# A choice of experts by sixteen compare-and-multiply instructions, with pinned transposes and three pairs of GpSimd work

## The chip, the cores and the metric

One core of one Trainium2 chip runs the whole program once. The metric is the device time of an execution in microseconds (us); lower is better. The kernel before took 1800.45 us, the median of three runs (1798.29 to 1802.6). Engines: TensorE (PE in the rows, PEld its weight loads), VectorE (DVE), ScalarE (ACT), GpSimd (POOL) and SyncE (SP), which issues the loads.

## What is computed

Two transformer blocks in a row over 256 tokens of width 1024. The change touches only the last part, the layer with 16384 small experts (PEER):

```python
def peer_ffn(u, w_q, sub_keys, u_tab, v_tab):      # T=256, K=16, H=8
    q = (xt @ w_q).reshape(T, H, 2, 128)
    s = jnp.einsum('thcd,hcnd->thcn', q, sub_keys)
    top_s, top_i = lax.top_k(s, K)                  # of 128 keys, per head and half c
    cand = (top_s[:, :, 0, :, None] + top_s[:, :, 1, None, :]).reshape(T, H, K * K)
    cand_i = (top_i[:, :, 0, :, None] * 128 + top_i[:, :, 1, None, :]).reshape(T, H, K * K)
    best_s, best_j = lax.top_k(cand, K)
    expert = jnp.take_along_axis(cand_i, best_j, axis=-1)
    g = jax.nn.softmax(best_s, axis=-1)
    ...
    act = gelu(einsum(xc, u_tab[ec]));  out = einsum(gc * act, v_tab[ec])
```

## The kernel before

The kernel never gathers experts. It computes the activations of all 16384 experts for all tokens, as 64 **pairs** of 256 experts (the u-loop in `peer`, lines 1534 to 1563), multiplies them by a dense weight `H` that is zero for all experts not chosen, and then runs the v-loop over 128 blocks.

**A pair** is one 1 MB load `w` (tile of `peer_u_2`), cut in two halves of 1024 columns. Each half goes through `split` (line 135): ScalarE copies it to `hi` (float32r, L145), and `lo = w - hi` (L146) is a subtraction on VectorE, or on GpSimd when `gp` is true, which in the u-loop is `i < N_POOL` (line 1539, `N_POOL = 7` at line 40). Then eight calls of `mm3` (lines 153 to 155) make three matmuls each, so a pair has 48. `hi` and `lo` have three buffers each (line 1629). The sums go to PSUM tiles `acc` for even pairs and `oa` for odd ones, two of each, so pair i+4 reuses the tile of pair i.

**The choice** (`choice`, line 1414) is a generator of 24 steps, spread over pairs 0 to 8 (lines 1532 and 1551): after pair i, steps are taken until 24(i+1)/9 are done. Steps 0 and 1 form candidates (L1422 to L1426). Steps 2 to 9 find the best 16 of 80 for 8 heads and both token halves (`topk`, L1402 to L1406). Step 10 turns places into a row place `rf` and a column place `cf` (L1437 to L1448), and casts the indices to `xb` in bf16. Step 11 makes the gate weights: L1453 subtracts, ScalarE takes the exponential (L1456), L1458 to L1460 normalise, two TensorE transposes (L1464) turn them, and L1465 to L1469 split them in three bf16 parts `g3`. It is issued after pair 4. Steps 12 to 23 look up the index at each place: for each half j of the tokens and each c of the two keys, VectorE compares 128 places with 16 numbers (L1478, 2048 columns), multiplies by the indices (L1481) and sums over 16 (L1484); TensorE transposes (L1486) and ScalarE writes a half of `iT` or `jT` (L1487).

**The weights** (`weights`, line 1490) come in 64 groups of four tokens, from pair 9 on, each with a compare `ohb` (L1495, from `jT`), four `oha` (L1498, from `iT` and `g3`), 12 small matmuls (L1505) and copies to `H` (L1512, L1514). A pair that finds n tokens of weights done multiplies these by its activations (L1547) and writes the others plainly (L1549). Pair 10 is the first for which n is not zero: it uses the first group.

The order of the instructions on each engine is not that of the program text: the tile framework lays it out beforehand by a simulated timeline (line 1749), and each engine then runs its list in order. `after(a, b)` (line 281) tells it that `a` must not stand before `b` on the same engine; nothing waits at run time for that. `peer_subkeys_2` is held in `sk`, which is last read by the last head's scores (L1526), ahead of pair 1.

Of the kernel before, what the change touches and what calls it, by code (L numbers as in the profile page):

```python
# [13 lines left out]
BF16 = mybir.dt.bfloat16  # L14
I32 = mybir.dt.int32
U32 = mybir.dt.uint32
AF = mybir.ActivationFunctionType
ALU = mybir.AluOpType
AX = mybir.AxisListType
# [17 lines left out]

N_END = 3

N_POOL = 7  # L40


class _Kernel:
# [1296 lines left out]
    def peer(self):  # L1340
        nc, I, X, V = self.nc, self.I, self.X, self.nc.vector
# [7 lines left out]
        def part(n, dt=F32):  # L1349
            o = at[0]  # L1350
            at[0] += n
            return ce[:, o:o + n].bitcast(dt) if dt is not F32 else ce[:, o:o + n]

        sk = part(2048).rearrange("p (n c) -> p n c", n=16)
        nc.sync.dma_start(sk, I["peer_subkeys_2"])
        xe = part(2048)
# [24 lines left out]
        def h_tile(first):  # L1381
            H.append((first, 32, big("H").rearrange("p (i t) -> p i t", i=32)))

        def rows_h(i, n):
            base, _, h = [z for z in H if z[0] <= i][-1]
            return h[:, i - base:i - base + n, :]
# [8 lines left out]
        xb = part(256, BF16).rearrange("p (j n a) -> p j n a", j=2, n=16)  # L1395
# [3 lines left out]
        def topk(v, ix, src):  # L1399

            scr = self.tmp([128, 128], "tk", bufs=2)[:, :src.shape[-1]]
            V.max(v[:, :8], src)  # L1402
            V.max_index(ix[:, :8], v[:, :8], src)
            V.match_replace(scr, v[:, :8], src, -3e38)
            V.max(v[:, 8:], scr)
            V.max_index(ix[:, 8:], v[:, 8:], scr)  # L1406
# [7 lines left out]
        def choice():  # L1414

            cand = xe[:, :1280].rearrange("p (j h n) -> p j h n", j=2, h=8)
            for j in range(2):
                va = v[j].rearrange("p (h c) a -> p h c a", c=2)  # L1420
                C = cand[:, j]
                V.tensor_tensor(C[:, :, :16], va[:, :, 0, 0:1].to_broadcast([128, 8, 16]), va[:, :, 1, :], op=ALU.add)  # L1422
                V.tensor_tensor(C[:, :, 16:72].rearrange("p h (a b) -> p h a b", a=7),
                                va[:, :, 0, 1:8, None].to_broadcast([128, 8, 7, 8]),
                                va[:, :, 1, None, :8].to_broadcast([128, 8, 7, 8]), op=ALU.add)
                V.tensor_tensor(C[:, :, 72:], va[:, :, 0, 8:], va[:, :, 1, 0:1].to_broadcast([128, 8, 8]), op=ALU.add)  # L1426
                yield
            bv4 = bv.rearrange("p (j h k) -> p j h k", j=2, h=8)
            bp4 = bp.rearrange("p (j h k) -> p j h k", j=2, h=8)
            for h in range(8):  # L1430
                for j in range(2):
                    topk(bv4[:, j, h], bp4[:, j, h], cand[:, j, h])
                yield

            u, rf, cf, m = [work[:, o:o + 256] for o in (0, 256, 512, 768)]
            ui = u.bitcast(U32)
            V.tensor_scalar(ui, bp, 3, None, op0=ALU.logical_shift_right)  # L1437
            V.tensor_copy(rf, ui)
            V.tensor_scalar(ui, bp, 7, None, op0=ALU.bitwise_and)
            V.tensor_copy(cf, ui)  # L1440
            V.scalar_tensor_tensor(m, rf, 9.0, cf, op0=ALU.is_equal, op1=ALU.mult)
            V.tensor_scalar(u, rf, 1.0, 8.0, op0=ALU.is_equal, op1=ALU.mult)
            V.tensor_tensor(cf, cf, u, op=ALU.add)
            V.tensor_tensor(cf, cf, m, op=ALU.subtract)
            V.tensor_scalar(rf, rf, -1.0, 0.0, op0=ALU.add, op1=ALU.max)
            V.tensor_tensor(rf, rf, m, op=ALU.add)
            for j in range(2):
                V.tensor_copy(xb[:, j], ix[j])  # L1448
            yield

            best, wt = bv.rearrange("p (n k) -> p n k", k=16), xe[:, :256]
            bw = wt.rearrange("p (n k) -> p n k", k=16)
            V.tensor_tensor(bw, best, best[:, :, 0:1].to_broadcast([128, 16, 16]), op=ALU.subtract)  # L1453
            for j in range(2):
                js = slice(j * 128, (j + 1) * 128)
                nc.scalar.activation(wt[:, js], wt[:, js], AF.Exp, scale=rs[:, j:j + 1])  # L1456
            z = self.small(16, "tk_z", bufs=1)
            V.tensor_reduce(z, bw, axis=AX.X, op=ALU.add)  # L1458
            V.reciprocal(z, z)
            V.tensor_tensor(bw, bw, z[:, :, None].to_broadcast([128, 16, 16]), op=ALU.mult)  # L1460
            pt = self.wk()[:, :256]
            for j in range(2):
                js = slice(j * 128, (j + 1) * 128)
                nc.tensor.transpose(pt[:, js], wt[:, js], self.ident)  # L1464
            nc.scalar.activation(g3[:, 0], pt, AF.Copy)  # L1465
            V.tensor_tensor(u, pt, g3[:, 0], op=ALU.subtract)
            nc.scalar.activation(g3[:, 1], u, AF.Copy)
            V.tensor_tensor(m, u, g3[:, 1], op=ALU.subtract)
            nc.scalar.activation(g3[:, 2], m, AF.Copy)  # L1469
            yield  # L1470
            eq = xe[:, 1024:].bitcast(BF16)
            eq3 = eq.rearrange("p (n s) -> p n s", s=16)
            eq4 = eq.rearrange("p (h k s) -> p h k s", h=8, k=16)
            for j in range(2):
                js = slice(j * 128, (j + 1) * 128)
                xj = xb[:, j].rearrange("p (h c) a -> p h c a", c=2)
                for c, pos in enumerate((rf, cf)):
                    V.tensor_tensor(eq3, pos[:, js, None].to_broadcast([128, 128, 16]),  # L1478
                                    self.iota[:, None, :16].to_broadcast([128, 128, 16]), op=ALU.is_equal)
                    yield  # L1480
                    V.tensor_tensor(eq4, eq4, xj[:, :, c, None, :].to_broadcast([128, 8, 16, 16]), op=ALU.mult)  # L1481
                    yield
                    hf = u[:, c * 128:(c + 1) * 128]
                    V.tensor_reduce(hf, eq3, axis=AX.X, op=ALU.add)  # L1484
                    pt = self.wk()
                    nc.tensor.transpose(pt[:, :128], hf, self.ident)  # L1486
                    nc.scalar.activation(tabs[c][:, js], pt[:, :128], AF.Copy)  # L1487
                    yield

        def weights():  # L1490

# [26 lines left out]
        for h in range(8):  # L1518
# [4 lines left out]
            s = self.wk().rearrange("p (n c) -> p n c", n=4)  # L1523
# [5 lines left out]
            if h == 1:  # L1529
                xT = self.xpair(xs, g_ffn)  # L1530
        self.e_done = self.t_done = 0
        work_, n_top, i_top, i_end, n_g = choice(), 24, 9, 62, T // 4
        done = 0
        for i in range(64):
            ut = self.next_w()
            ps = (self.acc, self.oacc)[i % 2]().rearrange("p (e t) -> p e t", e=2)
            for e in range(2):
                hi, lo = [z.rearrange("p (k e) -> p k e", k=8) for z in
                          self.split(ut[:, e * 1024:(e + 1) * 1024], gp=i < N_POOL)]
                for k in range(8):  # L1540
                    self.mm3(ps[:, e, :], (hi[:, k, :], lo[:, k, :]), (xT[0][:, k, :], xT[1][:, k, :]),
                             k == 0, k == 7)
            n = self.t_done
            h2 = rows_h(2 * i, 2)
            if n:
                nc.scalar.activation(ps[:, :, :n], ps[:, :, :n], AF.Gelu)
                V.tensor_tensor(h2[:, :, :n], h2[:, :, :n], ps[:, :, :n], op=ALU.mult)  # L1547
            if n < T:
                nc.scalar.activation(h2[:, :, n:], ps[:, :, n:], AF.Gelu)  # L1549
            self.e_done = 2 * i + 2  # L1550
            if i < i_top:
                want = n_top * (i + 1) // i_top
            else:
                want = n_top + n_g * (i + 1 - i_top) // (i_end - i_top)
            while done < min(want, n_top + n_g):
                if done == n_top:
                    for _ in work_:
                        raise AssertionError
                    h_tile(64)
                    h_tile(96)  # L1560
                    work_ = weights()
                next(work_)
                done += 1

        ps = [[self.acc() for _ in range(2)], [self.oacc() for _ in range(2)]]
# [29 lines left out]
        for i in range(128):  # L1595
# [8 lines left out]
            if i % 4 == 0:  # L1604
                ahl = self.act(F32R)
                ah, al = ahl[:, :1024], ahl[:, 1024:]
                a = rows_h(i, 4).rearrange("p i t -> p (i t)")
# [145 lines left out]
```

## Time and profile before

| | us |
|---|---|
| median of three runs | 1800.45 |
| lowest and highest | 1798.29 and 1802.6 |
| the profiled execution | 1797.24 |
| its span, first to last instruction | 1795.5 |
| TensorE busy | 1718.2 (96%) |
| VectorE busy | 982.3 (55%) |
| ScalarE busy | 683.0 (38%) |
| GpSimd busy | 309.9 (17%) |

The times in the rows are us from the start of the span. The u-loop runs from about 993 to 1430 us, the v-loop after it. In a timeline row, the first number is the start and the second the duration; successive instructions of one engine overlap a little, so the distance of two starts is what one costs its engine. Lines such as L146 or L153 are those of helpers and stand for every caller.

### The profile page before, as it was taken

To read this page: it belongs to the slowest core of one execution; us is meant where nothing else is said; L and a number is where in the kernel's file an instruction comes from. 1 tells how busy PE (TensorE), PEld (TensorE's weight loads), DVE (VectorE), ACT (ScalarE), POOL (GpSimd) and SP (SyncE) were. 2 spreads that over 40 slices of the span, in tenths; PEclk is the share of its full clock that TensorE was granted. 3 is DMA by queue.
4 is the path that set the end of the run, shared out by engine and by line. 5 is a ranking of instruction groups with operands and counts; after the bars stand their busy time and mean duration, and the time that the engine had idled before them with its cause. 6 is when DMAs were issued, how large, how long until landed. Compare 5 with 4: busy or idle time off the path is not lost. (4 is left out here: it accounts for less than half of the span.)

```text
span 1795.5 us, 27447 instructions
## 1 busy us (share of the span) xinstructions
PE 1718.2 (96%) x11096; PEld 1354.5 (75%) x11096; DVE 982.3 (55%) x2008; ACT 683.0 (38%) x1150; POOL 309.9 (17%) x178
## 2 busy tenths in 40 slices
PE   8999999999999998999999889999999999999998
PEld 7984445544434438888989889999999978888886
DVE  5462232212212116667566999999999944444444
ACT  6551121111101115546455444544444444444443
POOL 4321000000000005321537620000000022222221
PEclk9998999999999999999999989999999999999999
DMA  9527898898999978352215444444444455565553
GB/s 371 216 110 287 322 415 338 351 382 359 381 416 382 388 325 328 127 212 91 99 38 176 141 144 156 150 157 147 160 165 146 165 175 200 190 232 200 188 188 117
DMA packets 69250, 410.02 MB, mean 228 GB/s; under 512 B 9216, under 2 KB 9856, under 8 KB 28544
## 3 DMA queue, kind: packets, MB, share of 16 engines
q1 hardware_dynamic: 67840, 406.64, 60.4%
q8 instruction: 88, 1.44, 0.3%
q10 hardware_dynamic: 1280, 1.59, 0.2%
q14 instruction: 42, 0.34, 0.1%
HBM read 406.11 MB, written 2.10 MB: 227 GB/s over the span
## 5 line engine op out<-in xcount | busy, mean ns | idle before, releaser
L145 ACT ACTIVATE hi<-w 128x1024 fp32r<-128x1024 f32 x368 | 388.9, 1060 | 504.5 <-PE oa L155 176.9
L146 DVE TENSOR_TENSOR lo<-w,hi 128x1024 fp32r<-128x1024 f32 x260 | 327.2, 1260 | 222.0 <-ACT hi L145 221.7
L146 POOL TENSOR_TENSOR lo<-w,hi 128x1024 fp32r<-128x1024 f32 x108 | 267.2, 2476 | 1018.4 <-ACT hi L145 928.0
L155 PE MATMUL acc<-act,lo 128*128 128x256 f32 x928 | 267.0, 288 | 5.8 <-DVE lo L146 5.8
L153 PE MATMUL acc<-act,hi 128*128 128x256 f32 x928 | 266.3, 287 | 2.4 <-ACT hi L145 1.3
L154 PE MATMUL acc<-act,hi 128*128 128x256 f32 x928 | 264.0, 285 | 0.0
L757 PE MATMUL acc<-w,act 128*64 128x512 f32 x1016 | 246.6, 597 | 0.0
L154 PE MATMUL acc<-lo,act 128*128 128x256 f32 (+1 forms) x592 | 197.1, 333 | 3.0 <-POOL lo L146 1.6
L155 PE MATMUL acc<-hi,act 128*128 128x256 f32 (+1 forms) x592 | 195.8, 333 | 0.2 <-DVE act L1265 0.2
L155 PEld LDWEIGHTS acc<-act,lo 128*128 128x128 f32 x928 | 178.1, 192 | 9.3 <-DVE lo L146 6.6
L153 PEld LDWEIGHTS acc<-act,hi 128*128 128x128 f32 x928 | 178.3, 192 | 6.3 <-ACT hi L145 2.2
L153 PE MATMUL acc<-hi,act 128*128 128x256 f32 (+1 forms) x592 | 177.7, 335 | 1.8 <-ACT act L1608 1.0
L154 PEld LDWEIGHTS acc<-act,hi 128*128 128x128 f32 x928 | 178.3, 192 | 1.4 <-issue 1.2
L757 PEld LDWEIGHTS acc<-w,act 128*64 128x64 f32 x1016 | 73.3, 137 | 135.2 <-issue 131.3
L153 PE MATMUL oa<-act,hi 128*128 128x256 f32 x528 | 151.8, 288 | 4.0 <-ACT hi L145 3.9
L155 PE MATMUL oa<-act,lo 128*128 128x256 f32 x528 | 152.7, 289 | 0.0
L154 PE MATMUL oa<-act,hi 128*128 128x256 f32 x528 | 150.8, 286 | 0.0
L1498 DVE SCALAR_TENSOR_TENSOR oha<-cols,iT,g 128x384 bf16<-128x384 bf16 x256 | 142.3, 612 | 0.0
L154 PEld LDWEIGHTS acc<-lo,act 128*128 128x128 f32 x592 | 114.1, 193 | 16.5 <-DVE lo L146 3.5
L153 PEld LDWEIGHTS acc<-hi,act 128*128 128x128 f32 x592 | 114.1, 193 | 13.3 <-ACT act L1608 1.2
L155 PEld LDWEIGHTS acc<-hi,act 128*128 128x128 f32 x592 | 113.8, 193 | 10.6 <-DVE act L1265 0.4
L779 PE MATMUL oa<-w,mo_h 128*64 128x512 f32 x480 | 113.1, 599 | 5.0 <-ACT mo_h L767 5.0
(424 smaller groups left out, 2587.6 us busy)
## 6 DMA issues: line engine op xcount, KB each, us to landing
w<-w_gate SPq DMA_DIRECT2D x64, 1024.0 KB, 8.5
w<-peer_u SPq DMA_DIRECT2D x64, 1024.0 KB, 4.9
w<-peer_v SPq DMA_DIRECT2D x64, 1024.0 KB, 4.9
w<-w_up SPq DMA_DIRECT2D x63, 1024.0 KB, 9.5
w<-w_down SPq DMA_DIRECT2D x60, 1024.0 KB, 8.7
w<-w_in SPq DMA_DIRECT2D x28, 1024.0 KB, 9.2
w<-w_out SPq DMA_DIRECT2D x8, 1024.0 KB, 16.1
w<-peer_wq SPq DMA_DIRECT2D x8, 1024.0 KB, 4.8
```

The costliest lines, as they stand in the source:

```text
L145: self.last_hi = nc.scalar.activation(hi, src, AF.Copy)
L146: r = (nc.gpsimd if gp else nc.vector).tensor_tensor(lo, src, _f(hi), op=ALU.subtract)
L153: first = mm(ps, lhsT=a[0], rhs=b[0], start=start, stop=False)
L154: mm(ps, lhsT=a[0], rhs=b[1], start=False, stop=False)
L155: return first, mm(ps, lhsT=a[1], rhs=b[0], start=False, stop=stop)
L757: nc.tensor.matmul(ps[nm][e * 64:(e + 1) * 64, :], lhsT=xe[kh][:, k, s0:s0 + CAP], rhs=w[e][:, k, :], start=(kh + k == 0), stop=(kh * 4 + ...
L779: nc.tensor.matmul(y[hf][e * 64:(e + 1) * 64, :], lhsT=hT[:, kh * 2 + k, e * 64:(e + 1) * 64], rhs=w[e][k][:, hf * 512:(hf + 1) * 512], st ...
L1498: V.scalar_tensor_tensor(ab[:, t], cols[:, None, :].to_broadcast([128, 3, 128]), iT[:, t0 + t:t0 + t + 1], g3[:, :, t0 + t:t0 + t + 1].to_ ...
```

## The change

`N_POOL` goes from 7 to 3, so the `lo` of pairs 3 to 6 is made by VectorE. The transposes of the gate weights and of the looked-up indices are pinned behind `last_u`, the last matmul of the u-loop issued so far. The lookup is written anew: for each c, 16 instructions (one for each number s) compare all 256 places of both token halves with s and multiply by the index at s, into 16 rows of a bf16 tile that takes the place of `sk`; then sums of 8, 4, 2 and 1 rows add them up, and two transposes and one copy write all of `iT` (c = 0) or `jT` (c = 1). There are 24 steps as before: four steps of four instructions, one of sums and one of transposes for each c.

```diff
--- before.py
+++ after.py
@@ -37,7 +37,7 @@
 
 N_END = 3
 
-N_POOL = 7
+N_POOL = 3
 
 
 class _Kernel:
@@ -1461,31 +1461,34 @@
             pt = self.wk()[:, :256]
             for j in range(2):
                 js = slice(j * 128, (j + 1) * 128)
-                nc.tensor.transpose(pt[:, js], wt[:, js], self.ident)
+                self.after(nc.tensor.transpose(pt[:, js], wt[:, js], self.ident), self.last_u)
             nc.scalar.activation(g3[:, 0], pt, AF.Copy)
             V.tensor_tensor(u, pt, g3[:, 0], op=ALU.subtract)
             nc.scalar.activation(g3[:, 1], u, AF.Copy)
             V.tensor_tensor(m, u, g3[:, 1], op=ALU.subtract)
             nc.scalar.activation(g3[:, 2], m, AF.Copy)
             yield
-            eq = xe[:, 1024:].bitcast(BF16)
-            eq3 = eq.rearrange("p (n s) -> p n s", s=16)
-            eq4 = eq.rearrange("p (h k s) -> p h k s", h=8, k=16)
-            for j in range(2):
-                js = slice(j * 128, (j + 1) * 128)
-                xj = xb[:, j].rearrange("p (h c) a -> p h c a", c=2)
-                for c, pos in enumerate((rf, cf)):
-                    V.tensor_tensor(eq3, pos[:, js, None].to_broadcast([128, 128, 16]),
-                                    self.iota[:, None, :16].to_broadcast([128, 128, 16]), op=ALU.is_equal)
-                    yield
-                    V.tensor_tensor(eq4, eq4, xj[:, :, c, None, :].to_broadcast([128, 8, 16, 16]), op=ALU.mult)
-                    yield
-                    hf = u[:, c * 128:(c + 1) * 128]
-                    V.tensor_reduce(hf, eq3, axis=AX.X, op=ALU.add)
-                    pt = self.wk()
-                    nc.tensor.transpose(pt[:, :128], hf, self.ident)
-                    nc.scalar.activation(tabs[c][:, js], pt[:, :128], AF.Copy)
-                    yield
+
+            eq = sk.rearrange("p n c -> p (n c)").bitcast(BF16).rearrange("p (s n) -> p s n", s=16)
+            eq4 = eq.rearrange("p s (n k) -> p s n k", k=16)
+            x4 = xb.rearrange("p j (h c) a -> p (j h) c a", c=2)
+            for c, pos in enumerate((rf, cf)):
+                pos3 = pos.rearrange("p (n k) -> p n k", k=16)
+                for s in range(16):
+                    V.scalar_tensor_tensor(eq4[:, s], pos3, float(s), x4[:, :, c, s:s + 1].to_broadcast([128, 16, 16]),
+                                           op0=ALU.is_equal, op1=ALU.mult)
+                    if s % 4 == 3:
+                        yield
+                for n in (8, 4, 2):
+                    V.tensor_tensor(eq[:, :n], eq[:, :n], eq[:, n:2 * n], op=ALU.add)
+                V.tensor_tensor(u, eq[:, 0], eq[:, 1], op=ALU.add)
+                yield
+                pt = self.wk()[:, :256]
+                for j in range(2):
+                    js = slice(j * 128, (j + 1) * 128)
+                    self.after(nc.tensor.transpose(pt[:, js], u[:, js], self.ident), self.last_u)
+                nc.scalar.activation(tabs[c], pt, AF.Copy)
+                yield
 
         def weights():
 
@@ -1538,8 +1541,8 @@
                 hi, lo = [z.rearrange("p (k e) -> p k e", k=8) for z in
                           self.split(ut[:, e * 1024:(e + 1) * 1024], gp=i < N_POOL)]
                 for k in range(8):
-                    self.mm3(ps[:, e, :], (hi[:, k, :], lo[:, k, :]), (xT[0][:, k, :], xT[1][:, k, :]),
-                             k == 0, k == 7)
+                    self.last_u = self.mm3(ps[:, e, :], (hi[:, k, :], lo[:, k, :]), (xT[0][:, k, :], xT[1][:, k, :]),
+                                           k == 0, k == 7)[1]
             n = self.t_done
             h2 = rows_h(2 * i, 2)
             if n:
```

## Rows read from the trace of the kernel before

**Rows 1.** Page, slices of the span: TensorE's busy tenths and granted clock.

```profile
PE   8999999999999998999999889999999999999998
PEclk9998999999999999999999989999999999999999
```

**Rows 2.** Windows: length, busy (count) of PE PEld DVE ACT POOL, PEclk, DMA.

```profile
1020.00:1030.00 10.00, 5.02 (x42) 4.81 (x41) 9.93 (x88) 0.15 (x1) 0.87 (x1) 1.00 0.21 88
1030.00:1040.00 10.00, 5.00 (x24) 5.03 (x25) 9.90 (x15) 5.91 (x8) 6.70 (x3) 0.50 0.31 105
...
1050.00:1060.00 10.00, 7.16 (x49) 6.76 (x49) 10.00 (x14) 2.60 (x3) 0.00 (x0) 0.87 0.39 116
```

**Rows 3.** Timeline of TensorE: start, duration, instruction; pairs 0, 4 and 10.

```profile
993.25 0.28 PE L153 MATMUL acc<-act,hi 128*128 128x256 f32 x1
...
1022.70 0.28 PE L154 MATMUL acc<-act,hi 128*128 128x256 f32 x1
1022.82 0.28 PE L155 MATMUL acc<-act,lo 128*128 128x256 f32 x1
...
1076.11 0.29 PE L155 MATMUL acc<-act,lo 128*128 128x256 f32 x1
```

**Rows 4.** Windows over the choice and over the rest of the u-loop.

```profile
1001.00:1083.50 82.50, 69.01 (x540) 68.23 (x539) 81.27 (x205) 34.52 (x46) 26.68 (x10) 0.92 0.42 142
...
1090.00:1440.00 350.00, 343.95 (x3197) 338.16 (x3197) 332.59 (x585) 162.63 (x340) 0.00 (x0) 1.00 0.45 156
```

**Rows 5.** Waits from 970 to 1090: who for whom, us, times, longest.

```profile
ACT ce L1456 <- DVE ce L1453: 10.1, 1, 10.1
PE wk L1464 <- DVE ce L1460: 10.0, 1, 10.0
...
PE acc L155 <- DVE lo L146: 2.0, 1, 2.0
```

**Rows 6.** Timeline of VectorE in the choice.

```profile
1000.69 0.61 DVE L1423 TENSOR_TENSOR ce<-ce 128x448 f32<-128x448 f32 x1
...
1002.54 1.32 DVE L1422 TENSOR_TENSOR ce<-ce 128x128 f32<-128x128 f32 x1
...
1004.26 2.71 DVE L1423 TENSOR_TENSOR ce<-ce 128x448 f32<-128x448 f32 x1
...
1015.33 0.27 DVE L1422 TENSOR_TENSOR ce<-ce 128x128 f32<-128x128 f32 x1
...
1029.85 0.41 DVE L1453 TENSOR_TENSOR ce<-ce 128x256 f32<-128x256 f32 x1
...
1032.22 2.63 DVE L1460 TENSOR_TENSOR ce<-ce,tk_z 128x256 f32<-128x256 f32 x1
...
1040.84 3.11 DVE L1481 TENSOR_TENSOR ce<-ce 128x2048 bf16<-128x2048 bf16 x1
```

**Rows 7.** Timeline of GpSimd: the second half of pair 2.

```profile
1004.06 2.43 POOL L146 TENSOR_TENSOR lo<-w,hi 128x1024 fp32r<-128x1024 f32 x1 [0.34 <-ACT hi L145]
```

**Rows 8.** VectorE's groups, 1001 to 1083.5: count, busy us, mean ns, idle before.

```profile
L146 DVE TENSOR_TENSOR lo<-w,hi 128x1024 fp32r<-128x1024 f32 x13 | 15.7, 1219 | 1.0 <-ACT hi L145 1.0
L1478 DVE TENSOR_TENSOR ce<-ce,iota 128x2048 bf16<-128x2048 f32 x4 | 9.1, 2286 | 0.0
L1484 DVE TENSOR_REDUCE ce<-ce 128x128 f32<-128x2048 bf16 x4 | 9.1, 2280 | 0.0
L1481 DVE TENSOR_TENSOR ce<-ce 128x2048 bf16<-128x2048 bf16 x4 | 6.8, 1692 | 0.0
...
L1498 DVE SCALAR_TENSOR_TENSOR oha<-cols,iT,g 128x384 bf16<-128x384 bf16 x8 | 4.3, 609 | 0.0
...
L1441 DVE SCALAR_TENSOR_TENSOR ce<-ce 128x256 f32<-128x256 f32 x1 | 0.4, 381 | 0.0
```

**Rows 9.** Timelines of TensorE and VectorE: the last transpose and pair 10's product.

```profile
1087.85 0.27 PE L1486 MATMUL wk<-ident,ce 128*128 128x128 f32 x1
...
1092.84 0.16 DVE L1547 TENSOR_TENSOR H<-H,acc 128x8 f32<-128x8 f32 x1
```

## The prediction

> **What bounds the kernel now.** The profiled execution took 1797.24 us (span 1795.5), 3.2 us under the median of 1800.45 of the runs shown; I work out a saving in the profiled execution and take it off the median.
>
> I read the page's slices first (44.9 us each): TensorE is busy in nine tenths or more of nearly every slice, but less in the two from 987 to 1077 us, and in the second of them its granted clock dips too [rows 1]. That is where the edited code runs, so I opened that stretch in windows of 10 us. From 1020 to 1040 TensorE works half of the time, in 1030 to 1040 also at half clock (0.50), and it loses again in 1050 to 1060. VectorE is full in all of them [rows 2].
>
> What is lost, from the order of TensorE's work: a matmul starts every 0.12 us at full clock, so a pair of the u-loop (48 matmuls) needs 5.76 us. Pairs 0 to 4, with the last head's small matmuls between them, went from 993.25 to 1022.94, undisturbed. Six more pairs would end at 1022.94 + 6 x 5.76 = 1057.5; pair 10 in fact ended at 1076.23 [rows 3]. Taking 0.6 us for the six transposes, **18.1 us are lost**. That is the most that a repair here can give. From 1090 to 1440, TensorE is busy 344 of 350 us [rows 4], so little lies behind it.
>
> Why they are lost, from the waits: TensorE stood 10.0 us at the transposes of the gate weights (L1464) for VectorE's L1460, and ScalarE stood 10.1 us at the exponential (L1456) for VectorE's L1453, with the next `hi` copies queued behind it. Later 2.0 us went on a late `lo` [rows 5].
>
> VectorE was late for a reason that its own rows show. A 128x256 float32 operation on two tensors takes 0.41 us (L1453), but the same form at L1460 took 2.63 while GpSimd was in a `lo` subtraction; L1423 took 0.61 undisturbed and 2.71 beside GpSimd. There are eight lengthened instructions, from L1422 at 1002.54 (1.32, where its twin took 0.27) to L1481 at 1040.84 (3.11, where its three twins took 1.22) [rows 6, 8]. Against their undisturbed twins they took 15.7 us too long in all. The sizes agree: 9.4 us of it lie ahead of L1453 and 11.6 ahead of the transposes, which waited 10.1 and 10.0 us. My reading, which is an inference: the order of each engine was laid out for VectorE without these delays, and with engines that run in order, every delay of VectorE stops TensorE by nearly as much (10.0 of 11.6, so 1.6 us is forgiven).
>
> **The change part by part.**
>
> *GpSimd's share.* The pairs 3 to 6 lose GpSimd's `lo`, eight subtractions. GpSimd's last in this stage is then that at 1004.06 to 1006.49 [rows 7]. Of the 15.7 us of lengthening, the first two (L1422 and L1423: 1.05 + 2.10 = 3.15 us) fall before that and stay; 12.5 us go. In return VectorE does eight `lo` more: start to start one takes 1.14 us (1.22 busy [rows 8]), so 9.1 us. I take 3.15 for what stays, with bounds of 1 (one collision) and 5.4 (one 2.2 us collision more).
>
> *The values at places.* Removed: four each of L1478, L1481 and L1484, which start to start take 2.2, 1.13 and 2.2 us undisturbed, 22.1 in all [rows 8]. Added: 32 SCALAR_TENSOR_TENSOR of 256 columns. Nearest rows: L1441, the same form in float32, 0.38 us and 0.30 until the next begins; and L1498, the same operation with bf16 in and out and 384 columns, 0.61 long and 0.54 start to start [rows 8]. So 32 x 0.30 = 9.6 to 32 x 0.54 = 17.2; I take 0.36 (nearer L1441 by columns, and 0.54 x 256/384 = 0.36), 11.5. Two trees of sums, each of 2048, 1024, 512 and 256 columns: bf16 like L1481 gives 1.13 + 0.62 + 0.38 + 0.33 = 2.5; at the rate of L1478, 2.2 + 1.13 + 0.6 + 0.33 = 4.3. I take 2.5, as both operands are bf16 and contiguous, like L1481's output side. Sum: 16.5 (14.6 to 25.7) against 22.1.
>
> [...]
>
> *Order within it.* Before, the halves of tokens came one after the other: `iT` and `jT` of tokens 0 to 127 were there at step 17 of 24. Now `iT` is made for all tokens, then `jT`, so the first groups of `weights()` can only follow the last step. Pair 10 multiplies by the first group, and pair 14 reuses pair 10's PSUM bank, so **the end of the choice has a date: the start of pair 14**. Undisturbed that is 1022.94 + 9 x 5.76 + 0.6 = 1075.4.
>
> Does VectorE meet it? From 1001 to the end of its last choice instruction at 1083.5 it was busy 81.3 us [rows 4]. Of these, 13 `lo` (14.8), lengthening (15.7) and eight L1498 with two L1495 done early (5.4) come off: 45.4 is the choice and what was left of the heads, 23.3 without the 22.1. After: 23.3 + 16.5 + 3.15 + the 22 `lo` of pairs 3 to 13 (25.0) + early L1498 (4.2, at least 0) = 72.2, so the choice ends at about 1073.2. In before, 5.1 us lay between the last transpose and the end of the first L1547 [rows 9]; not all of that is work in a chain, and I take 4: 1077.2, a wait of 1.8 us at pair 14. Bounds: all small, 1066 or so, no wait; all large (25.7, 5.4, 5.1), 1089, a wait of 13 to 14.
>
> *The pins.* In before the transposes already stood behind the last matmul of the pair in which they are issued: L1464, issued in pair 4, ran 16 matmuls into pair 5. A pin that holds them there takes nothing away. I count it at nothing. It can't gain more than the 10.0 us at L1464 [rows 5], and those have another cause; it can cost where a transpose is held back by one pair, which delays only VectorE's two subtractions behind it and so part of the tail, at most as much as the wait found above at pair 14, 1.8 us, once more. Four ScalarE copies become two; ScalarE is under 60% busy here, so nothing.
>
> *Sum.* Lost after: lengthening that stays, 3.15 less 1.6 forgiven: 1.6; clock, where a wait of 10 us was followed by half clock over 5 us of matmuls (2.5 us lost) and one of 2.8 by about 1.3 us lost [rows 2]: 1.0; one late `lo` as in before: 2.0; pair 14: 1.8; of the 18.1, 0.9 that I can't place stays. Together 7.3, so 18.1 - 7.3 = 10.8 us less, and 1797.24 becomes 1786.4; from the median, **1789.6 us**.
>
> **The rivals.**
>
> *The wait at the exponential stays.* Ahead of L1453, 6.2 us of lengthening goes, and five `lo` (pairs 3, 4 and half of 5) come: 5.7. If the exponential keeps its place in ScalarE's order, it waits as long as before, and only L1460's 2.2 and 0.5 us come off the 10, and perhaps the later stall (4.1 with its clock). Then the saving is 2.7 to 7.5, about 5: 1795.5. For it: the balance of 6.2 and 5.7. Against: the new `lo` are known when the order is laid out, the lengthening (by my inference) was not.
>
> *VectorE becomes the bound at pair 14.* With the large ends above the wait is 13 to 14 us, and some 2 for the clock; of 18.1 about 2.6 is gained: 1798. For it: VectorE is at 9.9 to 10 of 10 us already [rows 2]. Against: it needs nearly all the upper bounds together.
>
> *Slower: `lo` behind the choice.* On GpSimd nothing stood ahead of the eight `lo`; on VectorE each can fall behind choice instructions, as the one at 1057 fell behind L1498 and cost 2.0 us of waiting [rows 5], 0.8 at the matmuls just before it and 1.3 of clock, 4.1. Five such late `lo` of eight are 20.5 us, more than the 18.1 that can be won; six cost 24.6 in place of 18.1 and give 1800.45 + 6.5 = 1807. It decides from five on. Against: with three `hi` buffers the copy of a block of 1024 columns may start two blocks, 5.8 us, ahead of its matmuls, and the added instructions are short (0.36 instead of 2.2), so that a `lo` stands behind less.
>
> **How the numbers follow.** Forecast 0.50, the wait stays 0.20, VectorE bound 0.15, late `lo` 0.15. A difference of 0.2% (3.6 us, about what a measurement of this kernel can tell from none) puts the border at 1796.9 and 1804.1. Faster: 0.50 + 0.16 + 0.06 = 0.72; same: 0.04 + 0.09 + 0.03 = 0.16; slower: the last rival's other 0.12. The forecast's own range is 1783 (a loss of 1 us left) to 1794; to hold 8 in 10 the whole goes to 1801, which takes in the first two rivals and leaves out most of the third.
>
> **What would show it.** In the profile after: no VectorE instruction of this stage over 2.4 us once GpSimd has ended at about 1006; the waits at L1456 and L1464 under 3 us each; no clock of 0.50 in a 10 us window; 32 instructions of 0.3 to 0.4 us; pair 14 beginning near 1077. It is wrong if the exponential still waits 8 us or more, if TensorE stands at several `lo`, or if the first L1547 comes after 1085.

## The result and the profile after

The changed kernel takes 1787.56 us (median of four runs, 1786.37 to 1788.57), the one before 1800.09 in the same comparison: a ratio of 0.9929 with a 95% interval of 0.9912 to 0.9946, so 12.5 us faster. Measured a second time among the experiments it was 1788.63 against 1799.73, 0.9937 (0.9923 to 0.9952), 11.1 us faster. The forecast was 1789.6, with 1783 to 1801.

The profiled execution took 1786.37 us (span 1784.7), 10.9 less than that of before. Its u-loop begins 1.6 us later, though nothing ahead of it was edited. So I measure the u-loop by itself, from the start of its first matmul to the start of its last. Before, that was 993.25 [rows 3] to 1436.15, **442.90 us**. After, from TensorE's timeline (start, duration, instruction):

```profile
994.83 0.28 PE L153 MATMUL acc<-act,hi 128*128 128x256 f32 x1
...
1425.28 0.28 PE L155 MATMUL oa<-act,lo 128*128 128x256 f32 x1
```

430.45 us, 12.45 less, close to the 12.5 between the medians. The same two rows in the second profiled execution of the changed kernel:

```profile
999.10 0.28 PE L153 MATMUL acc<-act,hi 128*128 128x256 f32 x1
...
1429.56 0.28 PE L155 MATMUL oa<-act,lo 128*128 128x256 f32 x1
```

430.46 us. The start wanders between executions (991.75 to 999.10 over all kernels here), while the u-loop's length agrees to 0.01 us in these two. It is the measure used below beside the medians; the other kernels have one profiled execution each. The two stretches as windows, before and after (columns as in rows 2):

```profile
993.25:1436.15 442.90, 424.39 (x3855) 418.43 (x3854) 421.03 (x827) 200.16 (x391) 31.52 (x12) 0.98 0.45 153
...
994.83:1425.28 430.45, 420.87 (x3855) 414.84 (x3854) 410.51 (x863) 200.09 (x389) 9.81 (x4) 1.00 0.46 157
```

So the 12.45 us are 8.9 less of idle TensorE (18.5 and 9.6) and 3.5 less in which its matmuls run, where before had the lowered clock of rows 2. In the changed kernel TensorE is busy in all but 9.6 us of its u-loop.

The stretch that was lost before [rows 2], in windows of 10 us (columns as there):

```profile
1020.00:1030.00 10.00, 10.00 (x84) 9.87 (x83) 10.00 (x56) 5.20 (x6) 0.00 (x0) 1.00 0.55 184
1030.00:1040.00 10.00, 10.00 (x86) 10.00 (x86) 9.93 (x38) 6.83 (x9) 0.00 (x0) 1.00 0.47 179
1040.00:1050.00 10.00, 8.73 (x73) 8.52 (x72) 10.00 (x23) 5.15 (x8) 0.00 (x0) 1.00 0.39 119
...
1080.00:1090.00 10.00, 8.54 (x84) 8.11 (x82) 10.00 (x21) 4.15 (x10) 0.00 (x0) 1.00 0.31 107
```

TensorE is full from 1020 to 1040, where it stood for half of the time, and the granted clock is 1.00 in every window. VectorE is as full as before. What is left of the waits from 970 to 1100 (the two of 10 us in rows 5 are gone):

```profile
PE acc L153 <- ACT H L1552: 1.5, 1, 1.5
...
PE acc L155 <- DVE lo L146: 1.3, 1, 1.3
...
PE oa L155 <- DVE lo L146: 1.0, 1, 1.0
...
PE oa L153 <- ACT hi L145: 0.8, 1, 0.8
```

4.6 us in four pieces. The gate weights wait for nothing any more. On ScalarE:

```profile
1032.79 0.58 ACT L1552 ACTIVATE H<-oa 128x512 f32<-128x512 f32 x1
1033.39 1.28 ACT L1456 ACT_TABLE_LOAD   x1
1034.69 0.70 ACT L1456 ACTIVATE ce<-ce,rs 128x128 f32<-128x128 f32 x2
1035.29 1.04 ACT L145 ACTIVATE hi<-w 128x1024 fp32r<-128x1024 f32 x1
```

The exponential stands behind the activation of pair 5 (`H<-oa` at 1032.79). In before it stood behind that of pair 3, two pairs earlier, and waited 10.1 us there:

```profile
1018.27 0.58 ACT L1549 ACTIVATE H<-oa 128x512 f32<-128x512 f32 x1
1018.87 1.28 ACT L1456 ACT_TABLE_LOAD   x1
1030.29 0.69 ACT L1456 ACTIVATE ce<-ce,rs 128x128 f32<-128x128 f32 x2 [10.14 <-DVE ce L1453]
```

On VectorE after the change, the lengthened and the formerly lengthened, and L1453, for which the exponential waits:

```profile
1004.12 1.32 DVE L1422 TENSOR_TENSOR ce<-ce 128x128 f32<-128x128 f32 x1
...
1005.83 2.70 DVE L1423 TENSOR_TENSOR ce<-ce 128x448 f32<-128x448 f32 x1
...
1008.73 0.28 DVE L1448 CAST ce<-ce 128x256 bf16<-128x256 uint32 x1
...
1034.23 0.41 DVE L1453 TENSOR_TENSOR ce<-ce 128x256 f32<-128x256 f32 x1
...
1036.95 0.42 DVE L1460 TENSOR_TENSOR ce<-ce,tk_z 128x256 f32<-128x256 f32 x1
```

The first two are as long as before [rows 6], since GpSimd still makes the `lo` of pair 2 beside them. Everything behind them is short: L1460 0.42 in place of 2.63. Yet L1453 comes no earlier. Counted from the start of the u-loop it ended at 37.0 us before [rows 6] and ends at 39.8 after, since the eight `lo` that were GpSimd's now stand ahead of it on VectorE. What moved is the exponential: its table load begins at 25.6 us before and at 38.6 after. So VectorE did not come sooner; ScalarE's order now asks for its result when it is there.

The new lookup, as groups of VectorE from 1001 to 1083.5 (columns as in rows 8):

```profile
L1478 DVE SCALAR_TENSOR_TENSOR ce<-ce 128x256 bf16<-128x256 f32 x32 | 11.2, 416 | 0.0
...
L1483 DVE TENSOR_TENSOR ce<-ce 128x2048 bf16<-128x2048 bf16 (+2 forms) x6 | 4.6, 771 | 0.0
```

### The profile page after: what moved, and what is told of

It is laid out like the page before. It is cut to its first block, busy times and chain, and to the rows that moved or that the text cites. A ratio compares the mean times of both kernels' runs of the same rounds, so it can differ in the third digit from the quotient of the medians.

```text
span 1784.7 us, 27473 instructions
## 1 busy us (share of the span) xinstructions
PE 1716.2 (96%) x11096; PEld 1352.5 (76%) x11096; DVE 971.5 (54%) x2044; ACT 682.9 (38%) x1148; POOL 287.9 (16%) x170
## 4 chain that ended last, share of the span: by engine, by line
PE 89%; DVE 7%; ACT 2%; issue 2%; POOL 1%; DMA 0%; ACTq 0%; POOLq 0%; DVEq 0%
PE acc L757 13%; PE acc L155 12%; PE acc L153 12%; PE acc L154 12%; PE oa L779 7%; PE oa L153 6%; PE oa L155 6%; PE oa L154 6%; PE wk L1508 2%; PE wk L711 2%; PE wk L713 2%; DVE lo L146 2%; PE wk L794 1%; PE wk L795 1%; ACT hi L145 1%
## 5 line engine op out<-in xcount | busy, mean ns | idle before, releaser
L146 DVE TENSOR_TENSOR lo<-w,hi 128x1024 fp32r<-128x1024 f32 x268 | 336.8, 1258 | 221.6 <-ACT hi L145 221.3
L146 POOL TENSOR_TENSOR lo<-w,hi 128x1024 fp32r<-128x1024 f32 x100 | 245.2, 2453 | 1029.5 <-ACT hi L145 943.6
```

Source lines behind the costliest of these rows:

```text
L146: r = (nc.gpsimd if gp else nc.vector).tensor_tensor(lo, src, _f(hi), op=ALU.subtract)
```

## The experiments

All times are medians beside runs of the kernel before on the same chip. "Length" is that of the u-loop in the profiled execution.

| kernel | us | before, us | ratio (95%) | length, us |
|---|---|---|---|---|
| before | | | | 442.90 |
| changed | 1787.56 | 1800.09 | 0.9929 (0.9912 to 0.9946) | 430.45 |
| changed, again | 1788.63 | 1799.73 | 0.9937 (0.9923 to 0.9952) | 430.46 |
| three pairs on GpSimd alone | 1791.47 | 1798.76 | 0.9968 (0.9956 to 0.9979) | 436.06 |
| lookup and pins alone | 1796.44 | 1798.76 | 0.9985 (0.9975 to 0.9996) | 439.71 |
| changed, five pairs | 1791.27 | 1798.76 | 0.9958 (0.9943 to 0.9972) | 436.03 |
| changed, no pair | 1787.71 | 1798.76 | 0.9942 (0.9928 to 0.9957) | 432.70 |
| before, exponential later | 1794.37 | 1799.73 | 0.9976 (0.9964 to 0.9987) | 437.66 |
| changed, date one pair later | 1788.17 | 1799.73 | 0.9937 (0.9923 to 0.9952) | 431.08 |
| changed, most of the lookup left out | 1780.35 | 1799.73 | 0.9896 (0.9878 to 0.9915) | 423.58 |
| no pair, date one pair later | 1788.40 | 1800.29 | 0.9933 (0.9918 to 0.9949) | 431.07 |
| no pair, date two pairs later | 1788.32 | 1800.29 | 0.9937 (0.9924 to 0.9950) | 430.21 |

**The pins** needed no run. The kernel before with the pins added has the same list of instructions on every engine as without them, and so has the changed kernel when its pins are taken out. They are worth nothing in these two kernels; what they would do in another layout was not tried.

### GpSimd's share alone

```diff
-N_POOL = 7
+N_POOL = 3
```

on the kernel before.

> The kernel before with GpSimd's share at three pairs and nothing else (old lookup, no pins). Theory (the lengthening of VectorE's instructions beside GpSimd, which the laid-out order doesn't know, was the loss): 12.5 us of lengthening go, the exponential and the gate transposes wait under 3 us, and 8 to 13 us of the 12.5 that the whole change gave are there already; 1787 to 1792. Rival (the shorter lookup is what pays): VectorE gets 9.1 us more work and nothing shorter, so the time stays within 3 us of before, 1797 to 1803, and the exponential still waits 8 us or more.

It took 1791.47, at the upper edge of the theory's 1787 to 1792, beside 1798.76 for before: 7.3 us of the gain, a little under the 8 to 13 expected. The waits at the gate weights are gone, as in the changed kernel, and the exponential stands behind pair 5's activation here too. So the share alone moved it. But a wait came up that I had not expected here, at the last transpose of the old lookup (TensorE's timeline; the bracket gives the idle time before and its releaser):

```profile
1084.07 0.47 PE L1486 MATMUL wk<-ident,ce 128*128 128x128 f32 x1 [6.05 <-DVE ce L1484]
1084.34 4.19 PE L1505 MATMUL wk<-oha,ohb 128*128 128x128 bf16 x33
...
1089.84 0.39 PE L153 MATMUL acc<-act,hi 128*128 128x256 f32 x1 [0.78 <-ACT H L1549]
```

TensorE had done pairs up to 13, found the choice not finished, stood 6.05 us, ran the first groups with the clock down (0.66 in the window from 1080 to 1090), and began pair 14 at 1089.84. That is the date that I set for the new lookup's end, missed by the old one, which is longer.

### The lookup and the pins alone

```diff
-N_POOL = 3
+N_POOL = 7
```

on the changed kernel.

> The changed kernel with GpSimd's share put back at seven pairs: the new lookup and the pins alone. Theory: the lengthened instructions ahead of the exponential are still there (about 9 us), the waits at L1456 and L1464 are again 8 to 12 us, and the time is 1794 to 1803. Rival (the shorter lookup pays): VectorE has 5.6 us less to do than before and 9.1 less than in the changed kernel, so it is at least as fast as the changed one, 1783 to 1789.

1796.44: 2.3 us under before, as the theory had it, and 8 to 9 us over the changed kernel, which excludes the rival. The waits, from 985 on (TensorE's and ScalarE's lists), are those of rows 5 to the tenth:

```profile
PE wk L1464 <- DVE ce L1460: 10.0, 1, 10.0
...
ACT ce L1456 <- DVE ce L1453: 10.1, 1, 10.1
```

and so are the lengthened instructions ahead of the exponential (L1448) and of the transposes (L1460):

```profile
1007.36 2.35 DVE L1448 CAST ce<-ce 128x256 bf16<-128x256 uint32 x1
...
1032.43 2.62 DVE L1460 TENSOR_TENSOR ce<-ce,tk_z 128x256 f32<-128x256 f32 x1
```

The parts add up to more together: by length 6.8 (share) and 3.2 (lookup, pins) make 10.0, and the whole gives 12.45. The run before shows why: with the share alone TensorE meets the unfinished choice ahead of pair 14, and only then does a shorter lookup release it.

### Five pairs

```diff
-N_POOL = 3
+N_POOL = 5
```

on the changed kernel.

> The changed kernel with GpSimd's share at five pairs, a dose between. Theory: four lo (4.6 us) leave VectorE, and three to four more instructions beside GpSimd are lengthened by 2 us each, ahead of the exponential, unplanned: 1 to 6 us slower than the changed kernel, 1788 to 1794, and the wait at the exponential lies between that of three and of seven pairs. Rival (VectorE's load at pair 14 decides): 1 to 2 us faster, as the 1.5 us wait there goes.

1791.27, within the range, and 5.6 us longer in the u-loop. The wait at the exponential lies between, as expected, but near one end: at 8.9 us it is nearly that of seven pairs, for the same five instructions ahead of L1453 are lengthened (1.32, 2.71, 2.34, 2.20 and 2.48 us). What agrees with the waits is how many two-operand instructions and casts of VectorE fell beside GpSimd ahead of the exponential, not the number of pairs: five and 10.1 us with seven pairs, five and 8.9 with five, two and no wait with three, where the exponential also stands later. Here TensorE's wait does not show at the transposes but at a `lo`:

```profile
PE oa L155 <- DVE lo L146: 6.9, 1, 6.9
...
ACT ce L1456 <- DVE ce L1453: 8.9, 1, 8.9
```

The exponential holds ScalarE, the next `hi` comes late, with it the `lo`, and TensorE stands. The wait at pair 14 is gone, as the rival had it, but the time is longer and not shorter.

### No pair

```diff
-N_POOL = 3
+N_POOL = 0
```

on the changed kernel.

> The changed kernel with no lo of the u-loop on GpSimd. Theory: the 3.15 us of lengthening that was left go, six lo more on VectorE cost 6.8 us, so the choice ends about 3.7 us later and pair 14 waits up to 5 us in place of 1.5, while the 1.0 us wait of pair 3 goes: 0 to 4 us slower than the changed kernel, 1787 to 1791. Rival (GpSimd beside VectorE is the cost, whatever VectorE has to do): 1.5 to 3 us faster, 1784 to 1786.

No VectorE instruction is lengthened in this stage. The time is that of the changed kernel (1787.71 here, 1787.56 and 1788.63 there), the u-loop 2.25 us longer, as the theory has it: pair 3's wait is gone, and TensorE stands at the first groups instead, 2.67 us for `ohb` and four times for `oha`:

```profile
1078.71 1.51 PE L1508 MATMUL wk<-oha,ohb 128*128 128x128 bf16 x24 [2.67 <-DVE ohb L1498]
1080.87 0.34 PE L1508 MATMUL wk<-oha,ohb 128*128 128x128 bf16 x3 [0.65 <-DVE oha L1501]
```

The rival, 1.5 to 3 us faster, is excluded by the length, though not by the medians alone.

### The exponential later

On the kernel before:

```diff
-                want = n_top * (i + 1) // i_top
+                want = (2, 5, 8, 10, 11, 11, 15, 19, 24)[i]
...
-                nc.scalar.activation(wt[:, js], wt[:, js], AF.Exp, scale=rs[:, j:j + 1])
+                self.after(nc.scalar.activation(wt[:, js], wt[:, js], AF.Exp, scale=rs[:, j:j + 1]), self.last_hi)
```

> The kernel before (seven pairs on GpSimd, old lookup) with only the place of the gate weights changed: step 11 is issued after pair 6 and its exponential pinned behind the hi copies of pair 6, three blocks (8.6 us) later in ScalarE's order than before. No VectorE instruction is shortened. Theory (the loss at the exponential comes of an order laid out for an undelayed VectorE): L1460 and its neighbours are as long as before, but the exponential waits under 3 us, TensorE's 10 us at L1464 are gone, and pair 14 starts when VectorE's choice ends, at 1088 to 1091 in place of 1095.8: 1791 to 1796. Rival (the lengthened instructions cost TensorE their time wherever the exponential stands): the 10 us wait appears at another instruction and the time stays within 3 us of before.

1794.37, 5.4 us under before (by length 5.2). The exponential's table load begins 8.2 us later from the start of the u-loop (33.8 in place of 25.6), and it waits 2.0 us in place of 10.1. L1422, L1423, both L1448 and L1426 are as long as before, and L1453 ends at 37.0 us as before: the wait fell by as much as the place moved. Two expectations failed. TensorE's wait at L1464 shrank but did not go, and L1460 and its neighbours are short, as GpSimd had finished pair 6's `lo` when they ran:

```profile
PE wk L1464 <- DVE ce L1460: 6.3, 1, 6.3
...
ACT ce L1456 <- DVE ce L1453: 2.0, 1, 2.0
```

```profile
1028.00 1.28 ACT L1456 ACT_TABLE_LOAD   x1
...
1030.82 0.41 DVE L1453 TENSOR_TENSOR ce<-ce 128x256 f32<-128x256 f32 x1
...
1033.12 0.43 DVE L1443 TENSOR_TENSOR ce<-ce 128x256 f32<-128x256 f32 x1
...
1036.78 1.23 DVE L1481 TENSOR_TENSOR ce<-ce 128x2048 bf16<-128x2048 bf16 x1
...
1038.65 0.42 DVE L1460 TENSOR_TENSOR ce<-ce,tk_z 128x256 f32<-128x256 f32 x1
```

L1443, L1460 and L1481 were lengthened by 6.3 us in before, so this run changes two things: the place of the exponential, and that lengthening. The gain in time is within the theory's 1791 to 1796, and the rival's 3 us of before is excluded; pair 14 starts at 1092.13, a little behind the expected 1088 to 1091. So 5.2 of the 12.45 us could be had with the same instructions on every engine, but how much of them is due to the exponential's place alone stays open. That the place in the order decides how long a late result is waited for is shown for the exponential. For the transposes it stays an inference.

### The date one pair later

```diff
-        work_, n_top, i_top, i_end, n_g = choice(), 24, 9, 62, T // 4
+        work_, n_top, i_top, i_end, n_g = choice(), 24, 10, 62, T // 4
```

on the changed kernel.

> The changed kernel with the choice spread over ten pairs in place of nine, so that the first groups of weights are asked for one pair later and pair 11, not pair 10, is the first to use them: the date of the choice's end moves from pair 14 to pair 15. Theory: the 1.5 us wait of TensorE at pair 14 goes and nothing else changes: 0 to 2 us faster than the changed kernel, and TensorE waits for no weights. Rival (VectorE is the bound anyway): the same wait appears one pair later and the time stays.

The 1.5 us wait ahead of pair 14 is gone, and nothing is won: the length is 431.08 against 430.45. TensorE instead stood 1.5 us at small matmuls of later groups for ScalarE. By the medians the kernel is 0.5 us faster than the changed one (1788.17 against 1788.63), by length 0.6 slower: the theory's 0 to 2 us are not told from none. The rival has the time right and the place wrong.

### Most of the lookup left out

```diff
                 for s in range(16):
-                    V.scalar_tensor_tensor(...)
+                    if s == 0:
+                        V.scalar_tensor_tensor(...)
...
-                for n in (8, 4, 2):
-                    V.tensor_tensor(eq[:, :n], eq[:, :n], eq[:, n:2 * n], op=ALU.add)
-                V.tensor_tensor(u, eq[:, 0], eq[:, 1], op=ALU.add)
+                V.tensor_tensor(u, eq[:, 0], eq[:, 0], op=ALU.add)
```

on the changed kernel.

> The changed kernel with most of the lookup left out: one compare-and-multiply for each c in place of 16 and no tree, so the experts are not the reference's. VectorE has about 14 us less to do in the choice. Theory: only the waits that TensorE still has there can go, 1.0 at pair 3, 1.3 and 0.8 at late lo and 1.5 at pair 14, so 1 to 4.5 us faster than the changed kernel, 1783 to 1787. Rival (VectorE's whole time in the choice sets the end): about 14 us faster, 1774.

8.3 us faster than the changed kernel in the second measurement (1780.35 against 1788.63), 6.9 by length: between the theory's 1 to 4.5 and the rival's 14. About half of VectorE's time taken out comes back. The named waits explain 3.5 of it: 1.27, 0.79 and 1.46 go. Another 1.4 is fewer waits behind 1100 us (5.0 in all in the changed kernel, 3.6 here). The other 1.9 is no wait: TensorE is busy 419.0 us here and 420.9 in the changed kernel, with the same matmuls. It stands five times in place of ten, and behind each of the changed kernel's ten the second matmul started 0.22 us after the first, where others start 0.12 apart: 0.1 us more each, which makes 0.5 for five; the rest I can't place.

### No pair, and the date later

The changed kernel with `N_POOL = 0` and `i_top` 11, then 10.

> The changed kernel with no lo of the u-loop on GpSimd and the choice spread over eleven pairs, so that the date of its end moves from pair 14 to pair 16. Theory: with no lengthening left the order laid out is met, the 1.0 us wait of pair 3 goes, and the 4 to 5 us that no GpSimd alone lost at the date (TensorE waiting at the first weights) go as well: the u-loop, 430.5 us in the changed kernel and 432.7 with no GpSimd, takes 426 to 430, and the time is 1783 to 1788. Rival (VectorE's load is the bound): the wait appears again at the later date, 1787 to 1791.

> The same with the choice over ten pairs, the date at pair 15. Theory: between, the u-loop 428 to 431 us and the time 1785 to 1789. Rival (VectorE's load is the bound): the u-loop as with no GpSimd alone, 432.7, and 1788 to 1791.

430.21 and 431.07 us of u-loop, 1788.32 and 1788.40: the time of the changed kernel. The lengths end just past the theory's 426 to 430 and 428 to 431; the times lie within the rival's ranges, but not its places. TensorE's waits for VectorE at the first groups shrank from 3.9 us to none and 1.1, and waits for `hi` and for ScalarE's copies, spread over later pairs, came in their place. Together with the run above: moving a date only moves the wait, and taking work from VectorE gives a part of it back. That fits a reading in which VectorE's load over the whole u-loop (94% busy, 421.6 of 450 us from 990 to 1440) makes the last waits. It is not shown: VectorE was as busy before (425.3 of 450), and TensorE itself is busy in all but 9.6 of the 430.45 us. No version faster than the changed kernel was found among those that compute everything.

## Why the prediction was right

By its steps:

- *What is lost, and why.* Right. The 18.1 us shrank to 4.6 us of waits, and the wait at the exponential follows the lengthening ahead of L1453: 9.4 us and 10.1 (before, and lookup alone), five instructions of the same size and 8.9 (five pairs), 3.15 and none (changed, and share alone), none and none (no pair). The lengthening is only half of it: with the same 9.4 and the exponential placed 8.2 us later, the wait was 2.0. By my inference the order was laid out for VectorE without the delays; that the waits are a matter of the place in the order is shown for the exponential, not for the transposes.
- *The share.* Right. L1422 and L1423 stay lengthened by 1.05 and 2.09 us, those of the other six that are still there are at their twins' length.
- *The lookup.* 16.5 us forecast. The 32 instructions start 0.334 us apart, which is 10.7 (11.5 forecast); the two trees, 1.13, 0.61, 0.33 and 0.33 from start to start, are 4.8 (5.0). Together 15.5. One of the 32 takes 416 ns, where L1441 took 381 in before [rows 8], and within a run of them the next begins 0.08 us before its end.
- *The date at pair 14.* Half right. The choice ended at 1073.3 us (1073.2 forecast, though the u-loop began 1.6 later), and pair 14 did wait for it, 1.46 us of the forecast 1.8. But I had set undisturbed pairs against a tail of 4 us. In fact the first L1547 (now L1550) came 10 us behind the choice, and pair 14 started at 1084.74 and not near 1077:

```profile
1084.74 0.38 PE L153 MATMUL acc<-act,hi 128*128 128x256 f32 x1 [1.46 <-ACT H L1552]
```

  TensorE had used the time: 36 small matmuls of the first groups went ahead of pair 14 (24 at 1078.29, 12 at 1082.44). Two errors of the same sign, one on each side, cancelled; that the wait came out near the forecast is luck.
- *Late `lo`, and the clock.* I took 2.0 us for one late `lo`; there were two of 1.04 and 1.27 and a late `hi` of 0.79. I took 1.0 us for the clock; it was 1.00 in every window, and the longest wait was 1.5 us. The lengthening that stays was to cost 1.6 at the exponential; it cost 1.04 at pair 3, a wait that is gone in the kernel with no pair on GpSimd. The 0.9 us kept as not placed can't be told apart. Forecast 7.3 us lost against 4.6 in waits, a saving of 10.8 against 12.45: the mechanism right, the remainder a little too large. That the profiled execution took 1786.37, just the 1786.4 worked out for it, is luck too: the later start of its u-loop, 1.6 us, made up the difference.
- *The pins.* Right; the lists of instructions are the same without them.
- *The rivals.* "The wait at the exponential stays" fell: its place in ScalarE's order was not kept, it moved by two pairs with the share alone. The balance that spoke for it was real (eight `lo` came ahead of L1453 and not five, and it ended 2.8 us later than before); the argument against it decided. "VectorE becomes the bound at pair 14" did not happen to the changed kernel, but is what the share alone ran into (6.05 us), so I gave it too little weight as a reason for the lookup. "Late `lo`" came at a quarter to a third of its price and twice, not five times.
- *What the forecast did not have.* That the two parts need each other (6.8 + 3.2 by length, 12.45 together), and that less work on VectorE gives more than the named waits, 6.9 us in place of at most 4.5, as the kernel with most of the lookup left out shows.

## What to carry to other kernels

Here 9.4 us of lengthened instructions on VectorE were followed by a wait of 10.1 us on ScalarE, with the next `hi` copies behind the exponential in its list, and TensorE stood 10.0 us at the transposes; that the order was laid out without the lengthening is my inference. Where an order of instructions is laid out beforehand, compare each long instruction with its undisturbed twin in the same trace, sum up the difference ahead of each wait, and see whether the sums agree with the waits. The late result need not come sooner: here it came 2.8 us later than before, and no engine waited for it, as the consumer had moved. Then look for the next date that the late engine must meet, for that is where a second part of the change may earn its gain.

## What the runs showed of the hardware

- In before, eight instructions of VectorE that ran beside a GpSimd subtraction took 1.05 to 2.22 us longer than their undisturbed twins; one such subtraction takes 2.43 us. The shortest and the longest were lengthened alike: 64 columns at L1426 took 2.19 us where its twin took 0.22, and 2048 at L1481 3.11 where its twins took 1.22. GpSimd's subtraction was lengthened as well: in before, one that met L1478 (2.29 us, as long as its twins) took 4.48 us:

```profile
1038.39 4.48 POOL L146 TENSOR_TENSOR lo<-w,hi 128x1024 fp32r<-128x1024 f32 x1 [1.29 <-ACT hi L145]
```

- Not every instruction beside a subtraction was lengthened. Of the eight, six have two operands in SBUF (L1422, L1423, L1426, L1460, L1443 and L1481), and two are a cast with one (L1448): 2.35 and 2.48 us beside GpSimd in before, 0.28 in the changed kernel. The searches for maxima kept their 0.2 to 0.3 us in the same stretch, and L1466, with one operand in PSUM, took 0.42 us at 1040.50, within the row of that subtraction, and 0.42 in the changed kernel, with no subtraction beside it.
- In the u-loop of the changed kernel, behind each of ten waits of 0.4 to 1.5 us, the second matmul started 0.22 us after the first, where others start 0.12 apart; the granted clock was 1.00.
